# WKV recurrence: a pair's two heads as two 64x64 array tiles instead of one block-diagonal 128x128 operand

## The chip, the core and the metric

One core of one Trainium2 chip runs the whole kernel in one launch. The metric is the device time of an execution in microseconds (us); three runs of the kernel before took 1816.57, 1819.95 and 1820.1 us, median 1819.95.

## The reference, cut to what matters

The program is one inference step of a four-layer decoder trunk on 256 prompt tokens and 8 sequences of 8 sample tokens, width 1024. The layers' mixers are RG-LRU, Mamba-2, RWKV-7 and RG-LRU; each is followed by a squared-ReLU MLP. The change is in the RWKV-7 mixer, whose core is this recurrence over the tokens, for 16 heads of 64 channels with a 64x64 state S each:

```python
def step(S, inp):
    r_t, k_t, v_t, kk_t, a_t, w_t = inp
    sa = jnp.einsum("bhvk,bhk->bhv", S, kk_t)
    S = (S * w_t[:, :, None, :] - sa[..., None] * (kk_t * a_t)[:, :, None, :]
         + v_t[..., None] * k_t[:, :, None, :])
    return S, jnp.einsum("bhvk,bhk->bhv", S, r_t)
```

It starts from zero for the prompt and from the given states for the samples; the output goes through a norm over the head, a bonus term and a gate, and then through the output projection `w_out`.

## The kernel before, in words

Features stand on the 128 partitions, the 320 tokens on the free axis. The large products split both sides in two float32r parts and add three products (`mm3`, L403 to L405); the weights come as a stream of [128, 1024] chunks, each split once by ScalarE (L399) and VectorE (L400).

`wkv` treats two heads together, a pair: head 0 is on partitions 0 to 63, head 1 on 64 to 127, so there are 8 pairs. The prompt's 256 tokens are four chunks of 64, and a chunk is solved with matrices: a triangular 64x64 system is inverted, and the state goes from chunk to chunk. So that one 128x128 matmul does both heads, the operands are block-diagonal: `put_bd` copies each head's half into buffers (`z1` to `z3`) whose other blocks were zeroed once.

- `setup(i)` copies four operands of pair i to block-diagonal form (L1267), forms score matrices (L1272, L1292), masks them on VectorE (L1274, L1276, L1294, L1296) and transposes three operands with TensorE (L1288), with copies out of PSUM on ScalarE (L1289).
- `inverse(g)` doubles the inverse over six levels (three for the samples) in float16: products L1309 and L1319, a masked copy on VectorE (L1323), two more products, a copy on ScalarE (L1333, L1337); then one correction from a float32 residual (L1344 to L1350). The four chunks go as two units of two chunks, each with its own PSUM buffer.
- `chain(p)` goes through the four chunks: X (L1400, L1402), copy (L1404), S (L1406), copy (L1408), the new state (L1410, L1411, L1419) and the outputs (L1413 to L1416).
- `chain_sample(p)` does the same for the eight sample sequences. Its first products (L1360) already use 64x64 tiles of the array, one for each head.
- `finish(p)` is norm, bonus and gate.

The loop at L1462 emits in iteration i the chain of pair i-1, the inverse of pair i, the setup of pair i+1 and the finish of pair i-2. A scheduler merges these into one fixed order for each engine; an engine then executes its own order strictly, and waits at an instruction whose operand is late. A float32 product is one row of that order and two instructions (weight load and matmul, twice) in the trace; a float16 product is one. The output projection (L1479 to L1491) follows, and its first products fill in at the end of the recurrence.

Of the kernel before, what the change touches and what calls it, by code (L numbers as in the profile page):

```python
# [18 lines left out]
P = 128  # L19
D = 1024  # L20
NT = D // P
TP = 256
# [15 lines left out]
NCV = NXB - (CW - 1)  # L38

# [1 line left out]
def _constants():  # L41
# [28 lines left out]
    for nm, samp in (("p", False), ("s", True)):  # L70
        seq = np.ones((P, 64)) if not samp else (s[:, None] // TS == t[None, :] // TS)
        c["wa_" + nm] = (s[:, None] < t[None, :]) * seq
        c["wg_" + nm] = (s[:, None] <= t[None, :]) * seq
    q = r[None, :]
    rr = r[:, None]
    for w in (1, 2, 4, 8, 16, 32):
        c[f"woff{w}"] = np.eye(P) - 1.0 * ((rr // (2 * w) == q // (2 * w)) & (rr // w > q // w))
    c["woff1t"] = c["woff1"].T
# [54 lines left out]
def _weight_chunks(a):  # L133
    """Every large weight, cut in [128, 1024] chunks, in the order of use."""
# [78 lines left out]
# first chunks of the layers, and the chunks that stay in float32 (the last with a tile of its own)  # L213
# [54 lines left out]
def prepare(a):  # L268
    """All kernel inputs: the reference's arrays, laid out for the core."""
# [53 lines left out]
@with_exitstack  # L323
def tile_hybrid_trunk(ctx: ExitStack, tc: tile.TileContext, wall, wlora, xt, wdt_d, s0_d, k0_d,
# [39 lines left out]
    # -- the stream of weights: each chunk loaded once, split exactly into two float32r parts --  # L364
# [11 lines left out]
    def fill(n):  # L376
        """Load and split chunks ahead, up to n of them."""
# [29 lines left out]
    def order(last, nk, nm):  # L407
        """(k, m) of the products of a chunk; the last chunk finishes one output after the other."""
# [3 lines left out]
    def chunk_steps(pt, ah, al, start=True, stop=True, n=N, ahead=True):  # L412
        """pt[:, m, :n] += chunk[k, m].T @ (ah + al)[k], k over 8 tiles, m over 2."""
# [15 lines left out]
    def weave(*parts):  # L429
        """Emits the parts' steps side by side; each part is (steps, their number, first and last of its time)."""  # L430
# [7 lines left out]
    def chunk_mm2(pts, ah, al):  # L438
        """Two such products side by side, half of k at a time."""
# [20 lines left out]
    # -- norms --  # L460
    class Norm:
        """Sum of squares over the features, tile by tile; then 1/rms on all partitions."""
# [16 lines left out]
        def finish_wide(self):  # L479
            """The same on all partitions at once, where the rows are waited for."""  # L480
# [16 lines left out]
        def finish(self):  # L497
# [11 lines left out]
            # one Newton step  # L509
# [13 lines left out]
    class Prep:  # L523
        """The next sublayer's operand: x * w split in two, and its sum of squares."""
# [29 lines left out]
        def renorm(self, pool):  # L554
            """The normed rows themselves, split in two, in place."""
# [16 lines left out]
    # -- squared-ReLU MLP --  # L572
# [25 lines left out]
    def pad_views(t, nt):  # L598
        """[128, nt, NXB] -> (prompt tokens, sample tokens, sample state) views."""
# [4 lines left out]
    def smp(t):  # L604
        """sample columns of a convolution output [128, n, NXB] -> [128, n, 8, 8]."""
        return t[:, :, PADP:].rearrange("p n (b c) -> p n b c", b=NB)[:, :, :, :TS]

    # -- layer A: RG-LRU --
    def mixer_a(ia, prep, nxt):
        with ExitStack() as st:  # L610
# [16 lines left out]
            def coefficients():  # L627
                """4 softplus(-lambda), by an exact log1p, its negative, and half of the gates' biases."""
# [38 lines left out]
            def gates(q):  # L667
                """The two gates of four blocks, by way of tanh: ra = 2 r - 1, ix = 2 i xc, th = tanh(8 r softplus)."""
# [9 lines left out]
            def decay():  # L678
                """Decay a in ra, 1 - a^2 in th."""
# [6 lines left out]
            def recur(c):  # L686
                """Recurrence from the entry states."""
# [38 lines left out]
            # states after the last tokens  # L726
# [11 lines left out]
    def log1p_tail(pool, e, u, shape):  # L738
        """log1p(e) from e and u = fl(1 + e): log(u) * e / (u - 1), or e where u == 1."""
# [18 lines left out]
    # -- layer B: Mamba-2 --  # L758
    def mixer_b(prep, nxt):
        with ExitStack() as st:  # L760
# [17 lines left out]
            def steps(ip):  # L778
                """Step sizes and cumulative decays of all heads, heads on partitions."""
# [136 lines left out]
                # masked C B^T, transposed (j on partitions; the samples on the upper half)  # L916
# [7 lines left out]
                # decays exp(acs_i - acs_j), i >= j  # L924
# [14 lines left out]
                # sample: entry state, four sequences side by side on the columns of the array  # L939
# [11 lines left out]
                # states left behind  # L951
# [15 lines left out]
                # outputs of the two head pairs  # L967
# [588 lines left out]
```

## Time and profile before

| | |
|---|---|
| median of 3 runs | 1819.95 us |
| span of the profiled execution | 1814.1 us |
| median less span | 5.9 us |
| PE busy over the span | 1763.7 us, 97% |
| VectorE (DVE), ScalarE (ACT) busy | 1204.8 us, 1038.8 us |
| stage of the recurrence | about 1015 to 1217 us |
| its output projection, the rest of it | 1217 to 1248 us |

The span runs from the first to the last instruction of the profiled execution; its own time beyond the span is not listed, so the table has the distance from the span to the median of the runs. PE is TensorE's matmuls, PEld its weight loads, which run beside them. A matmul's duration is longer than the distance at which the next one starts, so the busy share of PE says less than start-to-start distances. "L1309" is line 1309 of the kernel.

### The profile page before, as it was taken

The numbers are of one execution on the slowest core, as the hardware profiler recorded it, in microseconds if no ns is written. First come the engines' busy times: TensorE is split into PE (matmuls) and PEld (weight loads), VectorE is DVE, ScalarE is ACT, GpSimd is POOL, SyncE is SP. The second block draws the span as 40 slices with busy tenths as digits, with TensorE's granted clock in tenths as the row PEclk, the third lists the DMA queues.
The fourth block names the chain that finished last, engine by engine and source line by source line (L and its number), as shares of the span: only waits on it lengthen the run. The fifth ranks groups of instructions, "written<-read, shape, count | busy, mean of one in ns | idle before, by whom it ended". The sixth has DMA issues, their size and how long they took to land.

```text
span 1814.1 us, 31583 instructions
## 1 busy us (share of the span) xinstructions
PE 1763.7 (97%) x12650; PEld 1697.4 (94%) x12650; DVE 1204.8 (66%) x2113; ACT 1038.8 (57%) x1716; POOL 67.3 (4%) x86
## 2 busy tenths in 40 slices
PE   8999999989999999999999899999999999999997
PEld 7899999989999989999989788889999999899997
DVE  7965544699968965564586887777554458755434
ACT  7855433488858745553377877745553349555432
POOL 0000000000000000000000122120000000000000
PEclk9999999999999989999999999999999999999999
DMA  5444444546555534454423011023444444444442
GB/s 180 139 155 151 146 149 150 193 132 220 180 191 172 190 129 146 148 171 151 148 94 128 25 37 43 20 71 129 151 151 147 149 141 143 142 147 152 151 147 92
DMA packets 69858, 249.42 MB, mean 137 GB/s; under 512 B 9200, under 2 KB 11664, under 8 KB 67664
## 3 DMA queue, kind: packets, MB, share of 16 engines
q1 hardware_dynamic: 65168, 225.29, 37.8%
q0 software_dynamic: 2960, 18.89, 2.7%
q10 hardware_dynamic: 1584, 3.23, 0.5%
q8 instruction: 99, 1.62, 0.4%
q14 instruction: 47, 0.39, 0.1%
HBM read 233.46 MB, written 13.92 MB: 136 GB/s over the span
## 4 chain that ended last, share of the span: by engine, by line
PE 88%; DVE 7%; ACT 3%; issue 1%; DMA 1%; DVEq 0%; ACTq 0%; POOLq 0%
PE main_ps L403 22%; PE main_ps L404 22%; PE main_ps L405 22%; PE aux_ps L404 2%; PE aux_ps L403 2%; PE aux_ps L405 2%; PE ps_iv L1309 2%; DVE wlo L400 2%; PE aux_ps L673 1%; PE ps_cs L1386 1%; ACT z L1267 1%; DVE xc L697 1%; PE ps_cs L1360 1%; PE ps_cn L1411 1%; PE ps_sa L1288 1%
## 5 line engine op out<-in xcount | busy, mean ns | idle before, releaser
L399 ACT ACTIVATE whi<-wraw 128x1024 fp32r<-128x1024 f32 x401 | 424.2, 1059 | 599.9 <-PE main_ps L404 504.8
L400 DVE TENSOR_TENSOR wlo<-wraw,whi 128x1024 fp32r<-128x1024 f32 x401 | 489.9, 1223 | 361.6 <-ACT whi L399 352.6
L403 PE MATMUL main_ps<-xh,whi 128*128 128x320 f32 x1664 | 521.7, 313 | 15.3 <-ACT whi L399 7.9
L404 PE MATMUL main_ps<-xl,whi 128*128 128x320 f32 x1664 | 518.7, 312 | 0.0
L405 PE MATMUL main_ps<-xh,wlo 128*128 128x320 f32 x1664 | 516.5, 310 | 0.5 <-DVE wlo L400 0.5
L403 PEld LDWEIGHTS main_ps<-xh,whi 128*128 128x128 f32 x1664 | 314.6, 189 | 17.6 <-ACT whi L399 8.1
L404 PEld LDWEIGHTS main_ps<-xl,whi 128*128 128x128 f32 x1664 | 314.4, 189 | 2.1 <-issue 0.4
L405 PEld LDWEIGHTS main_ps<-xh,wlo 128*128 128x128 f32 x1664 | 314.3, 189 | 1.7 <-DVE wlo L400 1.1
L405 PE MATMUL main_ps<-hh,wlo 128*128 128x320 f32 x768 | 237.0, 309 | 0.9 <-DVE wlo L400 0.9
L403 PE MATMUL main_ps<-hh,whi 128*128 128x320 f32 x768 | 237.0, 309 | 0.2 <-ACT whi L399 0.2
L404 PE MATMUL main_ps<-hl,whi 128*128 128x320 f32 x768 | 236.9, 309 | 0.0
L405 PEld LDWEIGHTS main_ps<-hh,wlo 128*128 128x128 f32 x768 | 144.0, 187 | 1.2 <-DVE wlo L400 1.2
L403 PEld LDWEIGHTS main_ps<-hh,whi 128*128 128x128 f32 x768 | 144.0, 187 | 0.5 <-ACT whi L399 0.5
L404 PEld LDWEIGHTS main_ps<-hl,whi 128*128 128x128 f32 x768 | 144.0, 187 | 0.0
L583 DVE SCALAR_TENSOR_TENSOR fr<-main_ps,nrs 128x640 f32<-128x640 f32 x64 | 52.8, 824 | 78.5 <-PE main_ps L405 78.5
L403 PE MATMUL aux_ps<-hh,whi 128*128 128x320 f32 x256 | 79.0, 309 | 0.0
L405 PE MATMUL aux_ps<-hh,wlo 128*128 128x320 f32 x256 | 79.0, 309 | 0.0
L404 PE MATMUL aux_ps<-hl,whi 128*128 128x320 f32 x256 | 79.0, 308 | 0.0
L400 DVE TENSOR_TENSOR hl<-fh,hh 128x640 fp32r<-128x640 f32 x64 | 52.8, 825 | 13.0 <-ACT hh L399 13.0
L1323 DVE TENSOR_TENSOR wh<-ps_iv,k_c 128x256 f16<-128x256 f32 x108 | 44.6, 420 | 20.1 <-PE ps_iv L1309 17.9
L756 DVE SCALAR_TENSOR_TENSOR cv<-sxb,k_b,cv 128x344 f32<-128x344 f32 x96 | 51.7, 570 | 0.8 <-ACT cv L754 0.8
L585 ACT ACTIVATE fh<-fr 128x640 f32<-128x640 f32 x64 | 47.3, 739 | 7.0 <-DVE fr L583 7.0
(490 smaller groups left out, 3095.5 us busy)
## 6 DMA issues: line engine op xcount, KB each, us to landing
wraw<-in_wall SPq DMA_DIRECT2D x405, 512.0 KB, 3.3
ss<-in_s POOLq DMA_DIRECT2D x8, 1024.0 KB, 6.3
o_ssm_s<-ss POOLq DMA_DIRECT2D x8, 1024.0 KB, 4.4
acb<-acs_d SPq DMA_DIRECT2D x8, 640.0 KB, 3.8
k0t<-in_k SPq DMA_DIRECT2D x8, 256.0 KB, 2.8
o_wkv_s<-k0t SPq DMA_DIRECT2D x8, 256.0 KB, 2.0
o_ssm_p<-sp_o POOLq DMA_DIRECT2D x8, 128.0 KB, 4.0
wraw<-in_wlora SPq DMA_DIRECT2D x2, 512.0 KB, 3.3
```

The lines of the kernel that those rows point to most:

```text
L399: S.activation(hi, src, AF.Copy)
L400: V.tensor_tensor(lo, src, hi.bitcast(F32), op=ALU.subtract)
L403: T.matmul(out, wh, ah, start=start, stop=False)
L404: T.matmul(out, wh, al, start=False, stop=False)
L405: T.matmul(out, wl, ah, start=False, stop=stop)
L583: V.scalar_tensor_tensor(r, pt[:, :, :N], 0.0, b2(prep.rs), op0=ALU.max, op1=ALU.mult)
L585: S.activation(h, r, AF.Square)
L673: T.matmul(pt[:, :NCV], w4[:, h % 4, s], xc[:, h, :NCV], start=True, stop=True)
L697: V.tensor_tensor_scan(xc[:, h, :NCV], ra[:, h], ix[:, h], 0.0, op0=ALU.mult, op1=ALU.add)
L756: V.scalar_tensor_tensor(out, src[:, k:k + NCV], w[k], out, op0=ALU.mult, op1=ALU.add)
L1309: T.matmul(po[:, c * P:(c + 1) * P], l[:, c], r[:, c], start=True, stop=True)
L1323: V.tensor_tensor(h[k], q3(ph, 2), bc(vk(f"woff{b}"), 2), op=ALU.mult)
```

## The change

The block-diagonal buffers, `put_bd` and their zeroing go. Every product of a pair becomes two 64x64 products, one for each head, on its own half of the partitions (`both`). Operands that were 128 columns wide are 64 wide, and the float copies and masks work on the half width with both heads in one instruction. The operands of `setup` are read in place. The transposes become products with a 64x64 identity (`id64`). The inverse no longer goes in two units: all four chunks are one instruction on VectorE and ScalarE, with one PSUM buffer. The two score products of a mask are masked in one instruction (`wag`). The buffers of the weight stream, which held `ht`, `bt`, `vt` and `u`, are free during the recurrence, and those tensors have tiles of their own. The remaining differences are comments and constants of half the width.

```diff
+HEADS = (slice(0, 64), slice(64, P))
+            def both(po, l, r, start=True, stop=True):
+                for h in HEADS:
+                    T.matmul(po[h], l[h], r[h], start=start, stop=stop)
...
             def setup(i, samp):
-                for dst, src in zip((g.kb, bb, hb, vb), views):
-                    put_bd(dst, lambda o, r: S.activation(o, src[r], AF.Copy))
...
                 for c in range(n):
-                    T.matmul(pb[:, c * P:(c + 1) * P], bb[:, c], rhs[c], start=True, stop=True)
-                pb = q3(pb, n)
-                put_bd(g.ali, lambda o, r: V.copy_predicated(o, bc(ma[r], n).bitcast(mybir.dt.int32), pb[r, :, 0:64]))
+                    both(pb[:, c * P:(c + 1) * P], bb[:, c], rhs[c])
+                pb = q3(pb, n, P)
+                V.copy_predicated(g.ali, bc(ma, n).bitcast(mybir.dt.int32), pb[:, :, 0:64])
...
-                        T.transpose(pq[:, c * P:(c + 1) * P], src[:, c], ident)
+                            both(pq[:, o:o + 64], (hb, vb, bb)[k][:, c], vk("id64"))
...
             def inverse(g):
-                units = range(0, n, 2)
-                def mm2(po, l, r):
-                    for c in range(2):
-                        T.matmul(po[:, c * P:(c + 1) * P], l[:, c], r[:, c], start=True, stop=True)
+                def mm(po, l, r):
+                    for c in range(n):
+                        both(po[:, 64 * c:64 * c + 64], l[:, c], r[:, c])
...
             def chain(p, g):
-                    T.matmul(pX[:, :P], g.ak[:, c], g.vt[:, c], start=True, stop=s_ is None)
+                    both(pX, g.ak[:, c], g.vt[:, c], True, s_ is None)
...
-                    T.matmul(pS[:, :P], g.u[:, c], xs, start=True, stop=True)
+                    both(pS, g.u[:, c], xs)
```

The order on PE where the recurrence begins. `ps_sa` is the PSUM buffer of `setup`, `ps_iv` that of `inverse`; `z` is a block-diagonal buffer, `lw`, `av`, `vf` and `kr` the operands themselves. Before:

```order
L1188 MATMUL aux_ps<-wtmp,k_c 128x320
L1272 MATMUL ps_sa<-kr,z_10562 128x128 x4
L1288 MATMUL ps_sa<-k_cm,z_10562 128x128 x4
L1288 MATMUL ps_sa<-k_cm,z_10563 128x128 x4
L1288 MATMUL ps_sa<-k_cm,z_10562 128x128 x2
```

And now:

```order
L1189 MATMUL aux_ps<-wtmp,k_c 128x320
L1237 MATMUL ps_sa<-kr,lw_9274 64x128 x8
L1237 MATMUL ps_sa<-k_c,av_9278 64x64 x8
L1237 MATMUL ps_sa<-k_c,vf 64x64 x8
L1237 MATMUL ps_sa<-k_c,lw_9274 64x64 x7
```

The products are the same and stand in the same place; each is now two, and they read the operands without a copy in between.

The order on ScalarE over the same stretch; L1267 are the copies to block-diagonal form, `hbt`, `vut` and `tokp` the transposed operands, `warp` the system in float16. Before:

```order
L1110 ACTIVATE vf<-main_ps 128x640
L1232 ACTIVATE id_10574<-k_cm 128x128
L1267 ACTIVATE z_10564<-kr 64x2x64
L1189 ACTIVATE bs<-aux_ps 128x320
L1267 ACTIVATE z_10564<-kr 64x2x64
L1267 ACTIVATE z_10564<-lw_9274 64x2x64 x2
L1267 ACTIVATE z_10564<-av_9278 64x2x64 x2
L1267 ACTIVATE z_10564<-kr 64x2x64 x3
L1289 ACTIVATE hbt<-ps_sa 128x512
L1267 ACTIVATE z_10564<-kr 64x2x64
L1278 ACTIVATE warp<-ali_10572 128x512
```

And now:

```order
L1111 ACTIVATE vf<-main_ps 128x640
L1224 ACTIVATE id_10565<-k_c 128x64
L1190 ACTIVATE bs<-aux_ps 128x320
L1273 ACTIVATE tokp<-ps_sa 128x512
L1264 ACTIVATE warp<-ali_10562 128x256
L1273 ACTIVATE tokp<-ps_sa 128x256
L1316 ACTIVATE wutp<-ps_iv_10686 128x512
```

Nine copies are gone from between the last copy of the layer's projections and the first float16 system.

The order on PE in the chain of the last pair: `ps_cx` holds X and S, `ps_cn` the new state, `ps_po` the outputs, and the rows with `ylw` or `yav` are the output projection. Before:

```order
L1406 MATMUL ps_cx<-wxs,vut 128x128
L1367 MATMUL ps_cs<-svt,z_10564 128x128
L404 MATMUL ps_sa<-yav,whi 128x320
L405 MATMUL ps_sa<-ylw,wlo 128x320
L403 MATMUL ps_sa<-ylw,whi 128x320
L1442 MATMUL ps_iv_13693<-gsq,k_c 128x320
L1411 MATMUL ps_cn<-wsa,hbt 128x128
```

And now:

```order
L1237 MATMUL ps_cx<-wxs,wup 64x64 x2
L404 MATMUL ps_sa<-ylw,whi 128x320
L405 MATMUL ps_sa<-yav,whi 128x320
L406 MATMUL ps_sa<-ylw,wlo 128x320
L1237 MATMUL ps_cn<-wsa,tokp 64x64 x2
```

Work of the full array still stands between a chain's dependent products; but there the products before and behind it are on 64x64 tiles now, so that PE goes from one form to the other and back.

## Rows read from the trace of the kernel before

**Rows 1.** Part 1 of the page: busy us of each engine, share of the span, instructions.
```profile
PE 1763.7 (97%) x12650; PEld 1697.4 (94%) x12650; DVE 1204.8 (66%) x2113; ACT 1038.8 (57%) x1716; POOL 67.3 (4%) x86
```
**Rows 2.** Windows: stretch, length, busy us of PE, PEld, DVE, ACT, POOL, clock, DMA.
```profile
1015.00:1215.00 200.00, 195.04 (x1869) 168.37 (x1870) 150.21 (x385) 142.74 (x361) 45.32 (x48) 1.00 0.11 36
1215.00:1250.00 35.00, 33.27 (x209) 30.67 (x209) 27.35 (x50) 17.94 (x31) 1.04 (x1) 1.00 0.34 114
```
**Rows 3.** Groups by line and shape, 1014 to 1217 us: count | busy us, mean ns.
```profile
L1288 PE MATMUL ps_sa<-k_cm,z 128*128 128x128 f32 x120 | 21.4, 277 | 1.8 <-ACT hbt L1289 1.8
L1309 PE MATMUL ps_iv<-wut,wh 128*128 128x128 f16 x136 | 19.4, 219 | 0.0
...
L1400 PE MATMUL ps_cx<-vut,z 128*128 128x128 f32 x64 | 13.8, 297 | 0.0
...
L1292 PEld LDWEIGHTS ps_sa<-kr,z 128*128 128x128 f32 x80 | 10.4, 191 | 0.6 <-ACT vut L1289 0.2 <-ACT svt L1289 0.2
L1402 PE MATMUL ps_cx<-wsn,z 128*128 128x128 f32 x48 | 10.4, 298 | 0.0
L1309 PE MATMUL ps_iv<-wu,ali 128*128 128x128 f32 x64 | 10.3, 286 | 0.1
...
L1366 PE MATMUL ps_cs<-k_cm,z 128*128 128x128 f32 x16 | 3.5, 298 | 0.0
...
L1319 PE MATMUL ps_iv<-id,wars 128*128 128x128 f16 x8 | 1.3, 218 | 0.0
```
**Rows 4.** Timeline of PE, full array: start us, length us of the run, count.
```profile
1015.85 0.60 PE L1288 MATMUL ps_sa<-k_cm,z 128*128 128x128 f32 x4
...
1100.53 0.28 PE L1309 MATMUL ps_iv<-wut,wh 128*128 128x128 f16 x2
...
1101.43 0.30 PEld L1416 LDWEIGHTS ps_po<-gbtp,wsa 128*128 128x128 f32 x2
...
1105.39 0.97 PEld L1292 LDWEIGHTS ps_sa<-kr,z 128*128 128x128 f32 x8
```
**Rows 5.** The chain that ended last: start us, length us, PE's pieces.
```profile
1103.78 1.72 PE ps_cs L1386 x4
...
1177.84 0.54 PE ps_po L1436 x2
```
**Rows 6.** Timeline of PE around tiles of half the array.
```profile
942.70 0.42 PE L403 MATMUL main_ps<-loh,whi 64*128 64x320 f32 x2
...
1109.28 0.53 PE L1360 MATMUL ps_cs<-kr,k0t 64*64 64x16 f32 x12
...
1203.71 0.22 PE L1309 MATMUL ps_iv<-wt,wh 128*128 128x128 f16 x1
...
1203.86 0.23 PE L1360 MATMUL ps_cs<-kr,k0t 64*64 64x16 f32 x2
```
**Rows 7.** Single lines: count, then duration in ns, least/median/most.
```profile
L403 PE MATMUL main_ps<-loh,whi x16: 407/411/413, 940.1 to 948.0; 64*128 64x320 f32 x16
...
L1360 PE MATMUL ps_cs<-kr,k0t x256: 206/206/227, 1021.8 to 1204.8; 64*64 64x16 f32 x128
```
**Rows 8.** Groups of DVE and ACT by shape, 1014 to 1217 us.
```profile
L1323 DVE TENSOR_TENSOR wh<-ps_iv,k_c 128x256 f16<-128x256 f32 x108 | 44.6, 420 | 20.1 <-PE ps_iv L1309 17.9 <-PE ps_iv L1319 1.3
L1333 ACT ACTIVATE wut<-ps_iv 128x512 f16<-128x512 f32 x68 | 39.4, 594 | 14.1 <-PE ps_iv L1309 13.8
...
L1383 DVE TENSOR_TENSOR wex<-ssa,k_c 64x512 f32<-64x512 f32 x16 | 10.9, 683 | 0.2
...
L1267 ACT ACTIVATE z<-lw 64x256 f32<-64x256 f32 x14 | 5.8, 412 | 0.2
```
**Rows 9.** Timeline at the start of the recurrence; in brackets the idle time before.
```profile
1014.09 3.19 POOL L1234 COPY ali<-k_cm 128x512 f32<-128x512 f32 x2
...
1014.86 1.16 PE L1272 MATMUL ps_sa<-kr,z 128*128 128x128 f32 x8 [0.58 <-ACT bs L1189]
...
1018.04 0.85 PE L1288 MATMUL ps_sa<-k_cm,z 128*128 128x128 f32 x6 [1.59 <-ACT hbt L1289]
```

More of the change, by code (lines that the diff above doesn't have):

```diff
@@ L1275, in setup @@
+                pb = q3(pb, n, P)
+                V.copy_predicated(g.ali, bc(ma, n).bitcast(mybir.dt.int32), pb[:, :, 0:64])
                 g.gbt = qp.tile([P, n, 64], F32, name="gbt" + sfx)
                 V.tensor_tensor(g.gbt, pb[:, :, 64:128], bc(mg, n), op=ALU.mult)
[L1277 removed]
+                g.ar = qp.tile([P, n, 64], F16, name="war" + sfx)
                 S.activation(g.ar, g.ali, AF.Copy)
[L1279 to L1283 removed]
@@ L1290, in setup @@
+                g.ht, g.vt, g.bt = (g.tok[:, k] for k in range(3))
                 pz = ps("sa", 2)
                 for c in range(n):
-                    T.matmul(pz[:, c * P:(c + 1) * P], hb[:, c], rhs[c], start=True, stop=True)
-                pz = q3(pz, n)
-                put_bd(g.ak, lambda o, r: V.tensor_tensor(o, pz[r, :, 0:64], bc(ma[r], n), op=ALU.mult))
-                g.gkt = qp.tile([P, n, 64], F32, name="gkt" + sfx)
-                V.tensor_tensor(g.gkt, pz[:, :, 64:128], bc(mg, n), op=ALU.mult)
+                    both(pz[:, c * P:(c + 1) * P], hb[:, c], rhs[c])
@@ L1339, in inverse @@
[L1339 to L1350 removed]
+                iv = "iv0" if n == 4 else "iv2"
@@ new lines, in mm @@
+                def mm(po, l, r):
+                    for c in range(n):
+                        both(po[:, 64 * c:64 * c + 64], l[:, c], r[:, c])
+                t = qp.tile([P, n, 64], F16, name="wt1" + sfx, bufs=1)
+                V.tensor_tensor(t, g.ar, bc(vk("woff1t"), n), op=ALU.mult)
+                u = None
+                for b in g.levels:
+                    ph = ps(iv)
+                    if b == 1:
+                        for c in range(n):
+                            both(ph[:, 64 * c:64 * c + 64], g.ar[:, c], id16)
+                    else:
+                        mm(ph, g.ar, u)
+                    h = qp.tile([P, n, 64], F16, name="wh" + sfx)
+                    V.tensor_tensor(h, q3(ph, n), bc(vk(f"woff{b}"), n), op=ALU.mult)
+                    if b == 1:
+                        u = h
+                        continue
+                    pu = ps(iv)
+                    mm(pu, t, h)
+                    mm(pu[:, 64 * n:], h, t)
+                    last = b == g.levels[-1]
+                    ut = qp.tile([P, 2 * n, 64], F32 if last else F16, name=("wu0" if last else "wut") + sfx,
+                                 bufs=1 if last else 2)
+                    S.activation(ut, q3(pu, 2 * n), AF.Copy)
+                    u, t = ut[:, 0:n], ut[:, n:2 * n]
@@ L1380, in chain_sample @@
                     ex = qp.tile([P, NB, 64], F32, name="wex")
-                    for hh_ in range(2):
-                        r = slice(64 * hh_, 64 * hh_ + 64)
-                        (nc.gpsimd if f else V).tensor_tensor(
-                            ex[r], src[r, r].unsqueeze(1).to_broadcast([64, NB, 64]),
-                            vk("sbm")[r].unsqueeze(2).to_broadcast([64, NB, 64]), op=ALU.mult)
-                    T.matmul(pN, lt[:, j], ex.rearrange("p b v -> p (b v)"), start=f, stop=not f)
+                    (nc.gpsimd if f else V).tensor_tensor(
+                        ex, src.unsqueeze(1).to_broadcast([P, NB, 64]),
+                        vk("sbm").unsqueeze(2).to_broadcast([P, NB, 64]), op=ALU.mult)
+                    both(pN, lt[:, j], ex.rearrange("p b v -> p (b v)"), f, not f)
                 V.tensor_tensor(k0, k0, pN.rearrange("p (b v) -> p b v", b=NB), op=ALU.add)
@@ L1403, in chain @@
-                    xs = qp.tile([P, P], F32, name="wxs")
-                    S.activation(xs, pX[:, :P], AF.Copy)
-                    pS = ps("cx")
-                    T.matmul(pS[:, :P], g.u[:, c], xs, start=True, stop=True)
-                    sa = qp.tile([P, P], F32, name="wsa")
-                    S.activation(sa, pS[:, :P], AF.Copy, scale=-1.0)
-                    pN = ps("cn")
-                    T.matmul(pN[:, :P], g.ht[:, c], g.vt[:, c], start=True, stop=False)
-                    T.matmul(pN[:, :P], g.bt[:, c], sa, start=False, stop=True)
+                        both(pX, g.kb[c], s_, False, True)
@@ L1412, in chain @@
+                    xs = qp.tile([P, 64], F32, name="wxs")
+                    S.activation(xs, pX, AF.Copy)
+                    pS = ps("cx")[:, :64]
+                    both(pS, g.u[:, c], xs)
+                    sa = qp.tile([P, 64], F32, name="wsa")
+                    S.activation(sa, pS, AF.Copy, scale=-1.0)
+                    pN = ps("cn")[:, :64]
+                    both(pN, g.ht[:, c], g.vt[:, c], True, False)
+                    both(pN, g.bt[:, c], sa, False, True)
                     o = pO[:, 64 * c:64 * c + 64]
-                    T.matmul(o, g.vt[:, c], g.gkt[:, c], start=True, stop=False)
+                    both(o, g.vt[:, c], g.gkt[:, c], True, False)
@@ L1414, in chain @@
                     if s_ is not None:
-                        T.matmul(o, s_, kr[:, 1, p, 64 * c:64 * c + 64], start=False, stop=False)
-                    T.matmul(o, sa, g.gbt[:, c], start=False, stop=True)
-                    sn = qp.tile([P, P], F32, name="wsn")
+                        both(o, s_, kr[:, 1, p, 64 * c:64 * c + 64], False, False)
+                    both(o, sa, g.gbt[:, c], False, True)
+                    sn = qp.tile([P, 64], F32, name="wsn")
                     if s_ is not None:
-                        V.scalar_tensor_tensor(sn, pN[:, :P], dc, sd, op0=ALU.mult, op1=ALU.add)
+                        V.scalar_tensor_tensor(sn, pN, dc, sd, op0=ALU.mult, op1=ALU.add)
```

172 lines of the change are left out of this document (60 added, 112 removed).

## The prediction

> **What bounds the kernel now.** I read the page first, then windows, groups by shape, the timeline of PE, and the chain that ended last. PE is busy for 97% of the span [rows 1], and in the 200 us of the recurrence for 195 us at the full clock of 2.4 GHz, beside 150 us of VectorE and 143 us of ScalarE [rows 2]. So PE's own order sets the time here. But busy time counts a matmul to its end, while the next one starts earlier; what an instruction costs is the distance between starts. Eight weight loads of the setup take 0.97 us, one alone 0.191 [rows 3, 4], so (0.97 - 0.19) / 7 = 0.111 us for a float32 instruction of 128 weight columns. The load sets this, not the moving columns: L1416 streams half as many and two of its loads give 0.30 - 0.19 = 0.11 too. Transposes: (0.60 - 0.28) / 3 = 0.11. Float16: 0.28 - 0.22 = 0.06; I use 0.056, since rows are rounded and runs of eight give that or less. 512 moving columns: 1.72 / 4 = 0.43; 320 columns 0.54 / 2 = 0.27 [rows 5]. That is 0.84 ns for a float32 column.
>
> With the counts of the code (each float32 product is two instructions) the stage needs: 608 float16 instructions (68 for a pair's prompt, 16 for each of four sample groups; the first and the last of their forms are in [rows 3]) x 0.056 = 34 us; 800 float32 of one load each x 0.111 = 89 us; 120 transposes 13; 32 wide ones of L1386 14; 256 of L1360 at (0.53 - 0.21) / 11 = 0.029 [rows 6, 7], 7; norms, gates and two preparations, 56 x 0.27 = 15. Together 172 us. The other 28 of the 200 are waits and changes of form. Where PE goes from the full array to 64x64 tiles, starts are 0.15 us apart [rows 6] instead of 0.056, 0.09 extra; I take the same for the way back. The order has 56 such changes, 5 us. So about 23 us are waits.
>
> **The change part by part.** *Products with 64 moving columns or fewer.* These are 480 instructions of the chain (30 products a pair; L1400 has 64, L1402 48), 80 of the residual (L1309 in float32, 64 and 16), 80 of the sample chain (five lines like L1366), 640 in all [rows 3]. Each becomes two, one for each head. L1360 is the row that shows such tiles: 12 instructions in 0.53 us, and two start together and end together, 0.23 us for both against 0.227 at most for one [rows 6, 7]. So a pair of tiles goes every 2 x 0.029 = 0.058 us. L1360 moves only 16 columns; 64 need 64 x 0.84 = 54 ns, which still fits in 0.058 if the two tiles stream side by side. That they can, L403 on half the rows shows: two of 320 columns end 0.42 us after the first start, where one takes 0.411 [rows 6, 7]. Bounds: 0.058 for a pair, or 0.107 if the tiles stream one after the other. I take 0.058, the nearest row: 640 x (0.111 - 0.058) = -34 us.
>
> *Products that gain nothing.* The 160 instructions of the score matrices move 128 columns, 107 ns, as they do now; two tiles side by side keep 0.111. L1386 moves 512 and keeps 0.43. The 120 transposes become 480 tile instructions, 240 pairs x 0.058 = 13.9 against 13.2, +0.7 us. If tiles streamed in turn all three would lose; that is a rival below.
>
> *Float16 of the inverse.* 608 become 608 pairs. No row shows a 64-column float16 load. From below, streaming alone, 2 x 64 of the 128 columns that take 0.056 now in one matmul: with overlap 0.028 a pair, -17 us. From above, no overlap of two tiles' loads, 2 x 0.058 = 0.116, +36 us. L1360's loads overlap, so I take its 0.058: +1 us.
>
> The float16 loads of the full array are the shorter ones in the trace: their products stand 0.056 us apart, the float32 ones 0.111 [rows 3, 4]. The Trainium skill, page "TensorEngine Tiling (Array Packing)", section "Restrictions and Gotchas", says that column tiling excludes the fast weight load. By that rule the 64-column float16 load would cost as much as a float32 one of 64 columns, and the sum would be the one above; with a load that stays fast it would be up to 17 us lower. No row of before shows it.
>
> *Changes of form.* The new order has 78 in place of 56, because the output projection fills in between products that are tiles now: 22 x 0.09 = +2 us.
>
> *The start.* PE waits 0.58 us before the first score product and 1.59 us inside the transposes, for ScalarE, which copies operands to block-diagonal form, and the identity copies of POOL run until 1017.3 [rows 9]. Those ScalarE copies and the zeroing go, the POOL copies halve: -2 us (0 to -4).
>
> *ScalarE and VectorE.* The 96 block-diagonal copies of 0.3 to 0.41 us go, some 35 us of ScalarE; L1333's 68 copies become 32 of the same width and 4 of half, 19 us less; L1323's 108 become 60, 20 us or more less on VectorE; L1383 does both heads in one of its 0.683 us instead of two [rows 8]. All of it lies beside PE's work, so by itself it counts nothing; it shortens queues in front of dependent steps. Against that, the inverse is one chain for each pair instead of two units that fill each other's waits. One level is two hand-overs: a matmul's end (0.21), a masked copy of 0.42 and some 0.1 of semaphores; then a matmul's end, a copy of 0.594 and 0.1; about 0.73 and 0.9 us. Into these the new order puts setup and chain products of, by the distances above, mostly 0.5 to 1.3 us. Step by step the inverse falls short by some 12 us over all pairs and the chain by some 11; a wait of one fills a wait of the other, so I take 20 in place of 23: -3 us (bounds -12, all neighbours arrive early, and +25, waits double).
>
> *Sum.* -34 + 0.7 + 1 + 2 - 2 - 3 = -35 us. The order before and behind the stage is the same in both kernels, and the output projection's weights are no longer kept waiting for buffers that hold `hbt` and `vut`; what it does earlier only fills waits already counted. The span goes from 1814 to 1779; with the 5.9 us between span and median, 1785 us.
>
> **The rivals.** *Tiles that share a PSUM bank stream in turn* (slower). Both heads write the same bank, on different partitions. L403's two run side by side, but in two banks; L1360's are in one bank, but with 16 columns, 13 ns, it could hide a queue. For it: no row has two long streams into one bank. Against it: L1360's pairs have equal durations. The price: score products 160 x 0.111 = +18, L1386 32 x 0.43 = +14, transposes 240 x 0.107 - 13.2 = +12, the 640 no gain (-3), with changes of form and start 0: +41 us, 1861 us. It decides from the point where a pair of score tiles takes more than about 0.3 us; between, gain and loss cancel at roughly 0.16 for these and 0.08 for the narrow ones. The Trainium skill, page "TensorEngine Tiling (Array Packing)", "Gotcha 1: PSUM Pressure", says that different row tiles cannot access the same PSUM bank at once. Taken literally this is that rival; The trace neither bears it out nor excludes it: L1360's tiles start together in one bank, but move 16 columns.
>
> *Waits take the place of PE's work.* PE's needs fall to about 140 us, 17 a pair, and one pair's inverse alone is a chain of about 14 us. If half of the hand-overs are uncovered instead of a quarter, waits grow from 23 to 45: -35 + 25 = -10 us, 1810 us. For it: two units become one, and chain and inverse depend on each other from pair to pair. Against: the lists between dependent steps are about as long as the steps, and ScalarE and VectorE are shorter.
>
> *Float16 loads of two tiles do not overlap.* +36 - 1 on top of the forecast: no change, 1820 us. L1360's overlapping loads speak against it.
>
> *The tiles do better.* Float16 pairs at 0.028 and waits of 15: -35 - 18 - 5, 1762 us.
>
> **How the numbers follow.** The forecast, with gains of 20 to 52 us, has 0.66; waits 0.15; no overlap in float16 0.05; one bank 0.08; better 0.06. The likeliest time is 1785 us with a range of its own from 1768 to 1800. The range must reach into the waits rival: 1764 to 1810, which leaves out the bank, the float16 case and the extremes. A measurement of this kernel can tell 0.2%, 3.6 us, from no change. Faster: 0.66 + 0.15 + 0.06 less a little of the waits case, 0.86; same 0.05; slower, the bank and a remainder of others, 0.09.
>
> **What would show it.** Right: pairs of 64x64 products of `ps_cx`, `ps_cn` and `ps_po` start within 0.02 us of each other and pairs follow every 0.06 us; two tiles of 128 columns in `ps_sa` every 0.11; float16 pairs every 0.06; clock 1.00 through the stage; about 165 us from the first score product to the last chain; ScalarE near 70 to 80 and VectorE near 95 to 105 us of the stage. Wrong: if durations of the second tile are longer by the first one's stream, the bank rival; if PE has gaps in front of the inverse's products that ScalarE or VectorE ends, the waits; if the granted clock falls to 1.2 GHz in those gaps, more than all of these, since every distance above holds for 2.4 GHz.

## The result and the profile after

The changed kernel takes 1795.53 us (median of 4, 1794.56 to 1795.87), the kernel before 1819.82 us beside it: a ratio of 0.9864, 95% interval 0.985 to 0.9878, or 24 us faster. Forecast were 1785 us in a range from 1764 to 1810: a gain of 35 us in place of 24. The profiled execution has a span of 1794.1 us, 20.0 less than before, at a mean granted clock of 0.988 against 0.994; the rest of the 24 lies between the kernels' profiled executions and their medians (5.7 us before, 1.4 after). The 5.9 us that the forecast adds to its span are such a distance too: the profiled execution before was the fastest of its runs, 1816.57 us. The stage itself, from its first score product to its last product, went from 232.7 to 208.0 us, so the whole gain is there. It begins 3.7 us later in this execution, behind code that is the same in both kernels; one stretch there ran at 1.2 GHz only after the change (window 948 to 955 us of the changed kernel, columns as in [rows 2], the clock at 0.52 of full; 1.00 in the same window before):

```profile
948.00:955.00 7.00, 6.59 (x31) 5.80 (x32) 3.98 (x7) 6.85 (x15) 0.00 (x0) 0.52 0.01 2
```

Part 1 of the page of the changed kernel answers to [rows 1]:

```profile
PE 1742.8 (97%) x14450; PEld 1664.0 (93%) x14450; DVE 1150.2 (64%) x1984; ACT 969.6 (54%) x1560; POOL 49.5 (3%) x76
```

PE is still at 97%, with 1800 matmuls more. Two windows, first the stage before, then the stage after (length, busy us of PE, PEld, DVE, ACT, POOL with counts, clock, DMA share, GB/s), answer to [rows 2]:

```profile
1014.80:1247.60 232.80, 226.66 (x2064) 197.35 (x2064) 175.36 (x430) 158.46 (x388) 46.56 (x49) 1.00 0.15 49
```
```profile
1018.50:1226.60 208.10, 200.90 (x3864) 159.37 (x3864) 123.08 (x306) 93.84 (x247) 31.63 (x42) 0.98 0.18 56
```

ScalarE lost 65 us and VectorE 52; PE still reads as busy nearly all the time. That row misleads here, as the experiments show: a product that has only one half of the array at work reads as busy too.

The products are all on one line now, that of `both`. Timeline of PE in the changed kernel (start us, length us of the run, count), which answers to [rows 4 to 6]:

```profile
1018.57 1.09 PE L1237 MATMUL ps_sa<-kr,lw 64*64 64x128 f32 x16 [0.53 <-ACT bs L1190]
1019.50 0.63 PE L1237 MATMUL ps_sa<-k_c,av 64*64 64x64 f32 x16
...
1021.17 0.65 PE L1237 MATMUL ps_sa<-k_c,lw 64*64 64x64 f32 x14 [0.57 <-DVE gbtp L1262]
1021.65 0.31 PE L1237 MATMUL ps_iv<-id,warp 64*64 64x64 f16 x8
...
1075.96 0.31 PE L1237 MATMUL ps_iv<-wtp,whp 64*64 64x64 f16 x8 [1.25 <-ACT wtp L1323]
...
1122.71 0.33 PE L1237 MATMUL ps_cx<-wxs,wup 64*64 64x64 f32 x4
1122.87 0.29 PE L1237 MATMUL ps_iv<-whp,warp 64*64 64x64 f16 x8
```

One tile's matmul lasts 0.27 us with 128 float32 columns, 0.22 with 64, 0.19 in float16. So 16 score tiles go in (1.09 - 0.27) / 15 = 0.055 us each, 0.11 a pair; 16 transposes in (0.63 - 0.22) / 15 = 0.027, some 0.055 a pair; 8 float16 tiles in (0.31 - 0.19) / 7 = 0.017, 0.034 a pair. The tiles do run side by side, into one PSUM bank too.

In the same trace the wide products of the sample's state, which answer to the L1386 of [rows 5], look different:

```profile
1111.92 1.04 PE L1237 MATMUL ps_cs<-wex,toks 64*64 64x512 f32 x2
1112.58 0.44 PE L1237 MATMUL ps_iv<-wutp,warp 64*64 64x64 f16 x6
1112.86 0.62 PE L1237 MATMUL ps_cs<-wex,toks 64*64 64x512 f32 x1
1112.86 0.23 PE L1237 MATMUL ps_iv<-wutp,warp 64*64 64x64 f16 x2
1112.92 1.05 PE L1237 MATMUL ps_cs<-wex,toks 64*64 64x512 f32 x3
...
1114.00 0.62 PE L1237 MATMUL ps_cs<-wex,toks 64*64 64x512 f32 x1
...
1114.46 0.59 PE L1237 MATMUL ps_cs<-wex,toks 64*64 64x512 f32 x1
```

These are two products, each two passes of two halves: eight matmuls, which side by side would take 4 x 0.44 = 1.8 us. Here the first two passes stand alone, one behind the other, then come four as two pairs (one half of each product), then again two alone: 3.1 us from the first start to the last end. PE's queue shows why. The rows of the changed kernel at this place, in order, numbers left out (`ps_cs<-wex` is the sample's state product, each row one half; `ps_iv` the inverse of the next pair):

```
L1237 MATMUL ps_cs<-wex,toks 64x512
L1237 LDWEIGHTS warp
L1237 MATMUL ps_iv0<-wutp,warp 64x64
... (7 more of these two)
L1237 MATMUL ps_cs<-wex,toks 64x512
L1237 MATMUL ps_cs<-wex,toks 64x512
L1237 LDWEIGHTS wutp
L1237 MATMUL ps_iv0<-whp,wutp 64x64
... (7 more of these two, 8 of ps_iv0<-wutp,whp)
L1237 MATMUL ps_cs<-wex,toks 64x512
```

Each half is an instruction of its own, and the scheduler put the inverse, which has a high priority, between the two halves of a product. In the whole stage this holds for 203 of 1208 pairs, and for 15 of the 16 wide ones; of the 64 wide passes in the trace, 32 start with no other beside them.

A count over all starts of the stage sets a size to it: each matmul's form needs a distance to the next (0.029 us for a 64-column float32 tile, 0.055 for 128, 0.215 for 512, 0.016 in float16, the full-array forms as in the prediction, 0.147 in the output projection); what is left of the stage are waits, changes of form and, after the change, halves that stream alone; the count cannot tell these apart. Before, 200 us of the stage are such needs and 32 the rest; after, 152 and 55. PE's need fell by 48 us, more than forecast, and half of it came back in the rest. About 3.4 us of the 55 are a stretch at 1.2 GHz in this execution (windows further below). The stages of the other runs, where given below, had a clock of 1.00, so their distance to the changed kernel can hold that much of the clock.

### The profile page after: what moved, and what is told of

It is laid out like the page before. It is cut to its first block, busy times and chain, and to the rows that moved or that the text cites. A ratio compares the mean times of both kernels' runs of the same rounds, so it can differ in the third digit from the quotient of the medians.

```text
span 1794.1 us, 34846 instructions
## 1 busy us (share of the span) xinstructions
PE 1742.8 (97%) x14450; PEld 1664.0 (93%) x14450; DVE 1150.2 (64%) x1984; ACT 969.6 (54%) x1560; POOL 49.5 (3%) x76
## 4 chain that ended last, share of the span: by engine, by line
PE 88%; DVE 7%; ACT 2%; issue 1%; DMA 1%; POOL 0%; DVEq 0%; SPq 0%; ACTq 0%; POOLq 0%
PE main_ps L404 22%; PE main_ps L405 22%; PE main_ps L406 22%; PE aux_ps L405 2%; PE aux_ps L404 2%; PE aux_ps L406 2%; DVE wlo L401 2%; PE ps_sa L1237 2%; PE ps_cs L1237 2%; PE ps_iv L1237 1%; PE aux_ps L674 1%; PE ps_cx L1237 1%; PE ps_cn L1237 1%; DVE xc L698 1%; PE ps_po L1237 1%
## 5 line engine op out<-in xcount | busy, mean ns | idle before, releaser
L568 DVE TENSOR_TENSOR x<-x,main_ps 128x320 f32<-128x320 f32 x56 | 24.8, 484 | 36.9 <-PE main_ps L406 36.9
```

What stands on the lines that cost most here:

```text
L568: ins = V.tensor_tensor(x[:, i], x[:, i], half(pt, m)[:, :N], op=ALU.add)
```

## The experiments

Theory W: dependent steps (product, copy by ScalarE or VectorE, product) are uncovered now and set a pair's period. Theory P: PE's own work still sets the time. Theory T came after the first four runs: the split pairs are the loss. Ratios are against the kernel before, with 95% intervals; the changed kernel has 0.9864. Differences in us are those of ratios times 1819.8.

**More work for PE beside the chain.** `setup_twice_after` and `setup_twice_before`:

```diff
-                for c in range(n):
+                for c in list(range(n)) * 2:
```

> The changed kernel with the score products and the transposes of the setup issued twice into the same places (same values; the second pass overwrites the first). These instructions lie beside the inverse and the chain, not in them. The added work of PE is 320 64x64 products of 128 columns at 0.055 us and 480 of 64 columns at 0.029 us (start-to-start distances of the changed kernel's trace): 31.5 us. Theory W (the hand-overs of the dependent steps set a pair's period, PE waits 40 to 50 us of the stage anyway): well under half of it shows, +5 to +14 us against the changed kernel, a ratio of about 0.990 to 0.995 against the kernel before. Theory P (PE's own work, form changes and the half-clock stretch set the time): nearly all shows, +26 to +34 us, a ratio of 1.001 to 1.005.

> The kernel before with the same doubling: 160 block-diagonal products of 128 columns and 120 of 64 columns more, at 0.11 us each by its trace, +31 us of PE's work. Theory W holds that the kernel before was bound by PE there and became bound by waits only with the change: +22 to +33 us, a ratio of 1.012 to 1.018. Theory P expects the same here, +26 to +33 us. A rival to both, that waits set the time in the kernel before as well: under +12 us, a ratio below 1.007.

Measured: 1.0042 (1.0028 to 1.0055) and 1.02 (1.0185 to 1.0216), 32 and 36 us more than the same kernel without the doubling, for some 31 us of work each, so the whole price in both; the 36 lie above what either theory gave. W in its simple form falls: if the chain of hand-overs set the period, PE's waits would have swallowed part of it. But P does not explain the rest of 55 us either. By the same count it is 53 us with the doubling: work added elsewhere in the queue did not fill it. That the waits stand at fixed places in PE's queue is a reading of this, which no run shows by itself.

**The inverse's copy on two engines.** `split_copy`:

```diff
-                    S.activation(ut, q3(pu, 2 * n), AF.Copy)
+                    S.activation(ut[:, 0:n], q3(pu, n), AF.Copy)
+                    V.tensor_copy(ut[:, n:2 * n], q3(pu[:, 64 * n:], n))
```

> The changed kernel with the copy behind each level of the inverse split: the half that the next product reads first stays on ACT, the other half goes to DVE. No work of PE is changed. It shortens one hand-over of each level by about 0.1 to 0.2 us, 40 levels of the eight pairs. Theory W (the inverse's chain of hand-overs sets a pair's period): 3 to 8 us faster than the changed kernel, ratio 0.982 to 0.985 against the kernel before. Theory P: nothing, within 1.5 us of the changed kernel, ratio 0.9855 to 0.987; if DVE's queue delays its half, slower by a few us under either.

Measured: 0.9876 (0.986 to 0.9892), no different from the changed kernel. But the edit did not shorten the hand-over. One level of the changed kernel, the products, the copy and the next products, and then of this one:

```profile
1094.56 0.29 PE L1237 MATMUL ps_iv<-wutp,whp 64*64 64x64 f16 x8
1094.94 0.62 ACT L1316 ACTIVATE wutp<-ps_iv 128x512 f16<-128x512 f32 x1
1095.62 0.31 PE L1237 MATMUL ps_iv<-wutp,warp 64*64 64x64 f16 x8
```
```profile
1072.00 0.38 ACT L1316 ACTIVATE wutp<-ps_iv 128x256 f16<-128x256 f32 x1 [0.17 <-PE ps_iv L1237]
1072.42 0.42 DVE L1317 CAST wutp<-ps_iv 128x256 f16<-128x256 f32 x1
1073.53 0.31 PE L1237 MATMUL ps_iv<-wutp,warp 64*64 64x64 f16 x8
```

VectorE's half starts only when ScalarE's has ended, in all 48 copies. From the end of the products to the end of the copy the median of the pairs' 40 levels is 0.99 us instead of 0.64. So the run is the opposite of the test that its text names: hand-overs longer by 0.35 us, 14 us over the 40 levels. Its stage took 209.7 us at a clock of 1.00, about 5 us more than the changed kernel's 208.0 without the 3.4 us at 1.2 GHz. About a third of the longer hand-overs shows, which speaks against W in its full form; what a shorter one would give stays untested.

**Two inverses in flight.** `two_in_flight`:

```diff
-                iv = "iv0" if n == 4 else "iv2"
+                iv = g.iv          # iv0 or iv2 by the pair's parity
```

> The changed kernel with the inverses of even and odd pairs on PSUM buffers and SBUF tiles of their own, so that a pair's inverse need not wait until the one before has left its buffers; order of the code and work of PE unchanged. Theory W, in the form that one inverse in flight sets the period of a pair: 5 to 15 us faster than the changed kernel, ratio 0.978 to 0.984. Theory W in the form that the chain of the recurrence (which needs the inverse, and each chunk the one before) sets it: within 2 us. Theory P: within 2 us, ratio 0.9855 to 0.9875.

Measured: 0.9847 (0.9833 to 0.9862), some 3 us faster, with overlapping intervals: between the theories, so inconclusive by itself. Its stage took 204.5 us at a clock of 1.00, and the 3.4 us at 1.2 GHz, which it does not have, are as large as the difference. Repeated below without split pairs.

**The halves held together.** `halves_together`:

```diff
-                for h in HEADS:
-                    T.matmul(po[h], l[h], r[h], start=start, stop=stop)
+                h0, h1 = HEADS
+                a = T.matmul(po[h0], l[h0], r[h0], start=start, stop=stop)
+                with tc.issue_after(a.ins), tc.high_priority(2000):
+                    T.matmul(po[h1], l[h1], r[h1], start=start, stop=stop)
```

> The changed kernel with an order edge and a high priority on the second half of each 64x64 pair, so that it stands right behind the first in PE's queue; in the changed kernel the scheduler puts other products between the two halves of 203 of the 1208 pairs, of 15 of the 16 pairs with 512 columns among them. No product is added or removed. Theory T (a half that stands alone streams alone, and what is queued behind it waits for its part of the array): each split pair loses the overlap, 15 wide ones at up to 0.45 us, the other 188 at 0.03 to 0.06 us, 9 to 17 us in all: ratio against the kernel before 0.977 to 0.982. Theory W, now in the form that the waits at the hand-overs stay whatever the order of the halves: within 2 us of the changed kernel, 0.9855 to 0.9875.

Measured: 0.9762 (0.9748 to 0.9777), 1776.65 us, 19 us faster than the changed kernel with the same instructions, a little more than T's 9 to 17; without the 3.4 us at 1.2 GHz it is some 15. No pair is split in its order. Its stage as a window, against the window of the changed kernel above, and a wide product in its timeline (L1237 is the first half now, L1239 the second):

```profile
1018.80:1208.40 189.60, 183.30 (x3864) 148.49 (x3864) 123.39 (x306) 92.84 (x247) 31.65 (x42) 1.00 0.20 61
```
```profile
1061.82 0.61 PE L1237 MATMUL ps_cs<-wex,toks 64*64 64x512 f32 x1
1061.83 0.64 PE L1239 MATMUL ps_cs<-wex,toks 64*64 64x512 f32 x1
1062.27 0.59 PE L1237 MATMUL ps_cs<-wex,toks 64*64 64x512 f32 x1
1062.31 0.59 PE L1239 MATMUL ps_cs<-wex,toks 64*64 64x512 f32 x1
```

The halves start within 0.04 us of each other, two passes in 0.45 us for both heads. The stage is 18.5 us shorter, and PE's *busy* time fell by 17.6 of these: most of the loss had stood in the trace as work, not as a gap. The groups by line and shape (count | busy us, mean ns) of the wide products say the same, first of the changed kernel, then of this one:

```profile
L1237 PE MATMUL ps_cs<-wex,toks 64*64 64x512 f32 x64 | 24.8, 599 | 0.4 <-DVE kr L1350 0.3
```
```profile
L1239 PE MATMUL ps_cs<-wex,toks 64*64 64x512 f32 x32 | 15.8, 600 | 0.0
L1237 PE MATMUL ps_cs<-wex,toks 64*64 64x512 f32 x32 | 15.7, 596 | 0.1
```

The same 64 matmuls of the same 600 ns cover 24.8 us split, and some 16 side by side. The count over all starts leaves 37 us besides PE's needs, which are the same, so it falls by the 18.6 us of the stage. The edge and the priority also move other products; that the gain is the halves and not a luckier order is tested further below.

**Which pairs.** `wide_together` holds only the 16 wide pairs, `narrow_together` all but these:

```diff
-                    both(pN, lt[:, j], ex.rearrange("p b v -> p (b v)"), f, not f)
+                    both_tog(pN, lt[:, j], ex.rearrange("p b v -> p (b v)"), f, not f)
```

> The changed kernel with only the 16 pairs of 512 columns (the sample's state products) held together; 178 of the other pairs stay split. Halves_together gained 19 us. If a split pair costs what its half takes to stream alone (two passes of 0.22 us): 15 x 0.45 = 6.6 us faster than the changed kernel, ratio 0.982 to 0.984, and the rest of the 19 us belongs to the narrow pairs. If nearly all of the 19 us comes from the wide pairs, because what waits behind them is the inverse and the chain: 14 us or more faster, ratio below 0.979. If the wide ones are hidden in waits: within 2 us.

> The counterpart: all pairs held together but those of 512 columns, of which 9 of 16 are split in this order. By the price of a split wide pair (0.45 us) it is 9 x 0.45 = 4 us behind halves_together: ratio 0.977 to 0.980. If the wide pairs carry nearly all: 8 us or more behind, ratio above 0.9805. If the narrow ones carry all: level with halves_together, 0.9755 to 0.977.

Measured: 0.9807 (0.9792 to 0.9822), 10 us faster than the changed kernel, and 0.977 (0.9755 to 0.9784), level with `halves_together`. The 10 us of the wide pairs are the 6.6 us of their streams alone plus, as it seems, the 3.4 us at 1.2 GHz, which this kernel's stage (clock 1.00) does not have; yet the 9 that stay split in the second kernel cost almost nothing, though 24 of its 64 wide passes start alone. The two parts, 10 and 17 us, do not add up to 19: that each order has other neighbours is likely, but not shown. How the loss divides among pairs stays open.

**Halves set apart on purpose.** `setup_halves_in_turn`, on `halves_together`, a control for the other reading, that the scheduler had only found a luckier order:

```diff
-                for c in range(n):
-                    both(pb[:, c * P:(c + 1) * P], bb[:, c], rhs[c])
+                # in_turn: for h in HEADS, for each c: one matmul, queued behind the last
+                in_turn([(pb[:, c * P:(c + 1) * P], bb[:, c], rhs[c]) for c in range(n)])
```

> The kernel of halves_together with the setup's products in another order: all of a group's products on the first half of the partitions, then all on the second (groups of 4 to 16, held in a row by order edges). The same products in the same places, none depends on another. Theory T (two tiles run side by side only where the instruction next in PE's queue belongs to the other half): each group takes nearly twice as long. By the start-to-start distances of the changed kernel's trace (0.110 us for a pair of passes of 128 columns, 0.058 us of 64) a pair of groups of 128 columns costs 0.77 us more (16 of n = 4, 8 of n = 2 at 0.33), the transposes 1.28 us more a pair and 0.58 us a sample setup: 15 + 10 + 2, 27 us in all; 20 to 30 us slower than halves_together, ratio 0.987 to 0.993. Rival O (the gain of halves_together came from another order the scheduler happened to find, and where the halves stand does not matter): within 4 us of halves_together, ratio 0.974 to 0.979.

Measured: 0.9816 (0.9799 to 0.9832), 10 us slower than `halves_together`. Rival O, by which the place of the halves does not matter, is out, but the price is a third of the 27 us that T gave. Of the 10.8 us by which the stage is longer, PE's busy time has 9.3, and the setup's own products cover 54.7 us instead of 46.6; so the loss is in them, as T has it. The edges of this run also hold each group in a row, and no run does that with the halves side by side. Its timeline (L1247 is the first product of a group, L1250 the others) shows what T left out:

```profile
1017.31 0.43 PE L1247 MATMUL ps_sa<-kr,lw 64*64 64x128 f32 x2 [0.53 <-ACT bs L1190]
1017.58 0.98 PE L1250 MATMUL ps_sa<-kr,lw 64*64 64x128 f32 x11
1018.29 0.27 PE L1247 MATMUL ps_sa<-k_c,av 64*64 64x64 f32 x1
1018.40 0.27 PE L1250 MATMUL ps_sa<-kr,lw 64*64 64x128 f32 x1
1018.40 0.22 PE L1247 MATMUL ps_sa<-k_c,av 64*64 64x64 f32 x1
```

The next group's first half (`k_c,av`) starts at 1018.29 and 1018.40 beside the last passes of this group's second half: the two halves run a few instructions apart from each other here, and the shift is carried from group to group. So T stands with a correction: a pair may be split by a little. That it costs where a long stream or a wait lies between is how I read it, and no run tests it by itself.

**What is left.** Four variants of `halves_together`. `together_two_units` cuts the inverse back into two units (`units = [(k, f"iv{k}") for k in range(0, n, 2)]`, and each level runs over both); `together_two_in_flight` adds the buffers from above; `together_flight_heads` and `together_heads`, with and without these buffers, also make the finish's products with the block of ones tiles:

```diff
-                T.matmul(pm_[:, :N], vk("headones"), o, start=True, stop=True)
+                both2(pm_[:, :N], vk("headones"), o)    # one 64x64 tile for each head
```

> The kernel of halves_together with the inverse cut into two units of two chunks again, as in the kernel before: the same products, twice the hand-overs of half the size, which can cover each other. If the larger single unit of the change uncovers hand-overs of the inverse (theory W): 3 to 10 us faster than halves_together. If PE's work and its order alone count (theory T): within 2 us of halves_together. If the fixed cost of the 40 to 50 further instructions of ACT and DVE decides: 3 to 8 us slower.

> The kernel of halves_together with two_in_flight's buffers. Two_in_flight alone gained 5 us on the changed kernel. If the waits for the inverse's buffers and the split halves are separate losses, the gains add: 4 to 6 us faster than halves_together. If both are one loss (the order the scheduler finds): within 2 us of halves_together.

> The kernel of together_two_in_flight with the two products of the finish with the block of ones (320 columns, float32, block-diagonal 128x128) as two 64x64 tiles too. By the start-to-start distances of the changed kernel's trace a full-array pass of 320 columns between tiles costs 0.36 us and a pair of tile passes of 320 columns about 0.27 us; 32 passes and up to 32 form changes less. Theory F (form changes are paid one by one): 3 to 6 us faster than together_two_in_flight. If they are hidden in waits: within 1.5 us.

> The kernel of halves_together with the finish's products with the block of ones as 64x64 tiles, with the inverse's buffers as in the changed kernel. Together_flight_heads was 5 us faster than together_two_in_flight, which was level with halves_together. If the gain belongs to the ones' tiles alone: 3 to 6 us faster than halves_together, ratio 0.973 to 0.975. If it needs the second set of buffers: within 2 us of halves_together.

Measured: two units 0.98 (0.9785 to 0.9815), 7 us slower than `halves_together`: the one large unit of the change is right, the opposite of W, and more than T's 2 us. It is what the third expectation gives to the further instructions (412 instead of 357 on VectorE and 328 instead of 284 on ScalarE from 1015 to 1260 us); whether they or another order cost it is not separated. Two in flight 0.9762 (0.9746 to 0.9778), nothing. With the ones as tiles 0.974 (0.9726 to 0.9755) and, without the buffers, 0.9747 (0.9731 to 0.9763): 3 to 4 us better by the ratios, 4 to 5 by the medians, in the direction of theory F though not clear of the intervals. These two are the best versions, 1772.2 and 1772.3 us, against 1819.7 and 1819.0 of the kernel before beside them.

## Why the prediction was right in sign and range, and where it failed

*Products of 64 columns or fewer, -34 us*: right. Pairs go every 0.055 to 0.058 us, as taken from L1360.

*Score products, wide products and transposes, +0.7 us*: right where the halves stand together (0.11 us a score pair, 0.44 a wide pass in `halves_together`). The rival of the shared PSUM bank is out: 16 score tiles of 128 columns, of two row groups, go into one bank in 1.09 us, so two tiles do write it side by side. The Trainium skill, page "TensorEngine Tiling (Array Packing)", "Gotcha 1: PSUM Pressure", says that different row tiles cannot access one bank at once; the trace differs.

*Float16, +1 us*: mis-sized. A pair takes 0.034 us, not 0.058, near the lower bound of 0.028: 608 x (0.058 - 0.034) = 15 us more gain, a term of -13. I had taken the float32 row because no float16 row of that shape existed.

*Changes of form, +2 us*: right in count, too low in price. 56 changes became 77 (`together_heads` has 37). The 0.09 us hold for the way out of the full array; the way back, for which I had taken the same, costs 0.11 to 0.12 at the median of the starts, and the second pass of the full-array product behind it mostly comes another 0.10 late. By these prices the changes cost 7 us before and 12 after, +5.

*The start, -2 us*: half of it came. PE waits 0.53 us for ScalarE's `bs` before the first score product (0.58 in [rows 9]), and 0.57 for `gbtp` in the transposes in place of the 1.59. The first product of the inverse starts 3.1 us behind the first score product (1021.65 above) instead of 4.1:

```profile
1018.94 0.40 PE L1319 MATMUL ps_iv<-id,warp 128*128 128x128 f16 x4
```

This 1 us is in the count of the waits, so the sum below has 0 for it.

*Waits, 23 to 20, -3 us (bounds -12 and +25)*: this step failed. By the starts, what is left besides needs and changes of form went from 25 to 43 us, +18 (with the forecast's 0.09 for each change from 27 to 48). The forecast asked whether copies would be covered, step by step from durations, and took each product as one thing, whose two halves always run side by side. The size was that of the rival "waits take the place of PE's work", but its mechanism was not the main one: with the halves together 27 us are left of the 43, though every hand-over is in place; some 13 of these 16 us are split pairs and 3.4 the stretch at 1.2 GHz, and the 27 are near the 25 of before. `together_two_units`, with two units back, gives nothing back. The pairs that the order splits were to be seen before the run, in the order of the changed kernel, and I counted changes of form there but not this.

The sum by what was measured: -34 + 0.7 - 13 + 5 + 0 + 18 = -23 us, against -35 forecast and -24 timed. An error of 15 us in float16 met errors of 26 us the other way (waits, changes of form, start); the time lies in the range partly for that reason.

Of the signs named, the distances of the float32 pairs came out where the halves stand together, and so did ScalarE and VectorE (81 and 103 us to the end of the last chain). That end stands 180 us behind the first score product instead of 165; with the halves together it is 157.

*Clock*: the signs that would have made it wrong named a fall to 1.2 GHz. One came, once. Windows of the changed kernel:

```profile
1070.00:1074.00 4.00, 3.87 (x79) 2.70 (x78) 2.85 (x7) 1.26 (x4) 0.00 (x0) 1.00 0.57 201
1074.00:1078.00 4.00, 2.31 (x49) 1.57 (x45) 2.54 (x6) 3.03 (x7) 0.00 (x0) 1.00 0.31 74
1078.00:1082.00 4.00, 3.90 (x20) 2.06 (x22) 4.00 (x12) 1.07 (x4) 0.00 (x0) 0.50 0.38 127
1082.00:1085.00 3.00, 3.00 (x47) 2.92 (x45) 0.51 (x3) 1.75 (x4) 0.44 (x1) 0.53 0.80 236
1085.00:1090.00 5.00, 4.71 (x121) 3.79 (x119) 3.60 (x9) 1.68 (x5) 0.44 (x1) 1.00 0.18 71
```

PE was busy for 2.31 of 4 us, and then ran from 1078 to nearly 1085 at 1.2 GHz, where the 320-column product at 1078.10 lasted 1.44 us instead of 0.81. By the clock of these two windows that lost 2.0 + 1.4 = 3.4 us. It carries no more than a third of the 11 us that are missing from the forecast: `two_in_flight` ran its stage at a clock of 1.00 and needed 204.5 us for it, where 35 us less than before would be 198:

```profile
1017.90:1222.40 204.50, 198.04 (x3864) 155.30 (x3864) 123.10 (x306) 93.31 (x247) 32.83 (x42) 1.00 0.18 57
```

## What to carry to other kernels

A product cut into two tiles is two instructions, and a scheduler by priorities puts others between them here; look for the pairs' neighbours in the order, and hold them together with an edge. Busy time of PE does not tell a half-used array from a full one: compare a group's union of busy time with count times the distance of its form. What is left of the stage besides PE's needs is not slack: 31 us of added work cost 32 us beside 55 us of waits, changes of form and lone halves. And look in the trace whether an edit did what it was made for: the copy split over two engines ran one half behind the other.

## What the runs showed of the hardware that was not expected

Float16 tiles of 64x64 go in pairs every 0.034 us, 0.6 of the 0.056 of the full array's float16 product [rows 4]: two blocks on the diagonal are faster as tiles in float16 too, where I had expected no gain. The Trainium skill, page "TensorEngine Tiling (Array Packing)", section "Restrictions and Gotchas", excludes fast weight load under column tiling. The loads themselves are not much shorter than in float32, 107 ns against 138 (on the full array 102 against 191 [rows 3]), which does not speak against the rule; but the price that I had hung on it, 0.058 us a pair, did not appear:

```profile
L1309 PEld LDWEIGHTS <-warp 128*128 128x128 f16 x160 | 15.0, 102 | 5.1 <-issue 3.8
```
```profile
L1237 PEld LDWEIGHTS <-warp 64*64 64x64 f16 x384 | 17.0, 107 | 7.8 <-issue 7.1
L1237 PEld LDWEIGHTS ps_sa<-k_c,av 64*64 64x64 f32 x160 | 8.6, 138 | 1.3 <-issue 0.5 <-DVE sal L1260 0.4 <-DVE akgp L1280 0.3
```

The first product behind a change of form or a wait costs more than its distance: in the run of four at 1122.71 above, behind a full-array product, 0.33 - 0.22 = 0.11 us lie between the first and the last start, where four of the transposes need some 0.06; and the 14 transposes at 1021.17, behind a wait, have 0.43 between theirs, where 13 distances of 0.027 are 0.36.

A full-array product of 320 columns among tiles takes 0.37 us between the starts of its two passes (`ps_po<-go,gw` in the changed kernel), and the next tile starts 0.36 behind the second (1122.71 above): 0.74 in place of 0.54 by [rows 5]. Only the second of these can be put down to the change of form alone. In the kernel before, a product behind a wait, with the full array on both sides, is as long, and the next one starts 0.64 us behind it instead of 0.74:

```profile
1121.97 0.81 PE L1418 MATMUL ps_po<-go,gw 128*128 128x320 f32 x2
```
```profile
1133.14 0.81 PE L1442 MATMUL ps_po<-gsq,k_c 128*128 128x320 f32 x2 [0.15 <-ACT gsq L1440]
1133.78 0.28 PE L1309 MATMUL ps_iv<-wut,wars 128*128 128x128 f16 x2
```
